# Attention: reciprocals of the softmax's sums carried over the partitions by DMA, outputs multiplied and split by GpSimd

## The chip, the cores and the metric

The kernel runs on one core of one Trainium2 chip. A core has a matrix engine (TensorE, PE in the profile; PEld is its loading of weights), three engines for elementwise work (VectorE or DVE, ScalarE or ACT, GpSimd or POOL), and a queue engine SP from which nearly all DMAs of this kernel are issued. Each engine executes its own list of instructions in order, and waits where an instruction needs what another engine has not finished. The metric is the device time of one execution in microseconds.

## The reference, cut to what matters

One layer over 1024 latent tokens and 256 context tokens, width 1024, all in float32: a gated feed-forward half-step, then a short convolution and grouped-query attention side by side, merged and projected, then a second half-step and a norm. The change lies in the attention of the latent tokens:

```python
def gqa_attend(q, k, v):
    s = jnp.einsum('btkgd,blkd->bkgtl', q, k, preferred_element_type=jnp.float32) * (HEAD_DIM ** -0.5)
    p = jax.nn.softmax(s, axis=-1).astype(v.dtype)
    return jnp.einsum('bkgtl,blkd->btkgd', p, v)
...
x = x + ml[5] * merge_branches(y_conv_l, o_l, gt_l, w_branch_conv[layer], w_branch_attn[layer], w_out[layer])
```

There are 8 query heads of 128 channels, 2 key and value heads, and 1280 keys (256 of the context, 1024 latent). The kernel multiplies the unnormalized sums of values by the reciprocal of the softmax's sum afterwards, and that is where the change is.

## The kernel before, in words

Every product that needs float32 precision is made of three faster ones: an operand is split into a high part and a low part (`split`, line 197: ACT casts the high part, then DVE, or POOL where it is named, subtracts it from the source), and `mm3` (line 229) does high times high, high times low and low times high.

The attention is cut into 16 units (`Unit`, line 1501): 8 heads by two halves `C0` and `C1` of 512 tokens. A unit does the following.

- `begin`: splits its queries into two tiles `qs` of 512 columns.
- `scores`, four times, for 128 queries each: nine matmuls against all keys, maxima by DVE (`m`, `nm`), exponentials by ACT into `pc` (context) and `pl` (latent), whose sums DVE adds into one column of `rsum`. So `rsum` is [128 queries of a block, 4 blocks]: the queries stand on the partitions.
- `turn`, ten times, for 128 keys each: four PE transposes put the keys on the partitions in a PSUM tile `pt`, and `split` makes `pts` of it. `pt` tiles come from `ps_t`, which has two PSUM banks.
- `values`, ten times: three matmuls of 512 columns add to `po` (one bank): [128 channels, 512 queries].
- `output` (line 1558): here the queries stand on the free axis, so the reciprocals `rinv`, one a partition, must be turned and repeated on all 128 partitions. The kernel does this by four PE transposes of a broadcast column into a `pt` bank; ACT copies `po` into the head's tile `q`, whose queries are no longer needed, and DVE multiplies it by the bank.

`seconds` (line 1568) runs turns and values of a unit behind the scores of the next; values follow their turn by `AHEAD` = 3. Between them `fillers` (line 1623) put the convolution branch's projection: weights `wc` (their low part by POOL), inputs `y`, gate `g`, result to DRAM as `zd`. From unit 13 on, `split_output` (line 1495) splits one finished head of 1024 columns, `q`, into `oh` and `ol` twice a unit; head 6 and the two halves of head 7 are split behind the units. `merge` (line 1591) then reads all eight heads' `oh` and `ol` in eight steps of three matmuls, with `ga` and `z` loaded from DRAM. The merges of the first two column blocks are woven into the last unit's turns. `later_mod` steps (`rawm` loads, `macc` on DVE) belong to the next feed-forward and are run behind the attention.

The order of the work is not written out by hand. A planner goes through the program and sets each engine's order from its own estimate of times: an instruction goes as soon as its inputs and a free buffer are there, the earlier in the program first. Only instructions marked as pinned or strict keep their place. So the scores run units ahead of the turns, and an instruction can appear well before its place in the text. The buffers that matter here: eleven tiles of 512 columns (`tpool`, by `ttile`), for `qs`, `g`, `ga`, `z`, `rawm`, `macc` and others; four of each kind of `small` tile, among them `rinv`; 38 of 1024 columns (`atile`) for `q`, `pl`, `oh`, `ol`.

In the profile, nearly all instructions carry line 90, that of a helper which issues them, so tiles are named rather than lines.

Of the kernel before, what the change touches and what calls it, by code (L numbers as in the profile page):

```python
# [9 lines left out]
F32 = mybir.dt.float32  # L10
# [8 lines left out]
P = 128  # L19
# [7 lines left out]
NQ = 8  # L27
# [8 lines left out]
C0, C1, CC = ("l", 0, 512), ("l", 512, 512), ("c", 0, CT)  # L36
# [15 lines left out]
def tile_dit_layer(  # L52
# [44 lines left out]
    act, dve, pool, pe, sp = (Engine(e) for e in (nc.scalar, nc.vector, nc.gpsimd, nc.tensor, nc.sync))  # L97
# [7 lines left out]
    dram = ctx.enter_context(tc.tile_pool(name="dram", bufs=1, space=DRAM))  # L105
# [3 lines left out]
    def uniq(s):  # L109
        n_tiles[0] += 1  # L110
        return f"{s}_{n_tiles[0]}"

    def atile(name, shape=(P, SLOT), dt=F32):
        return apool.tile(list(shape), dt, tag="A", name=uniq(name))

    def ttile(name, n=512, dt=F32):
        t = tpool.tile([P, 512], dt, tag="t", name=uniq(name))
        return t[:, :n]

    def small(name, n, dt=F32):  # L120
        return spool.tile([P, n], dt, tag=f"s{n}_{name}", name=uniq(name))
# [4 lines left out]
    def ps_t(n=512):  # L126
        return psum.tile([P, 512], F32, tag="t", name=uniq("pt"), bufs=2)[:, :n]
# [4 lines left out]
    def matmul(out, w, x, start, stop, pinned=False, on=False):  # L132

        inst = pe.matmul(out, w, x, start=start, stop=stop, skip_group_check=on)
        if pinned:
            tc.keep_in_program_order(inst)

    def transpose(out, in_, pinned=False):
        n = in_.shape[0]
        inst = pe.transpose(out, in_, ident[:n, :n])  # L140
        if pinned:
            tc.keep_in_program_order(inst)
# [43 lines left out]
    def col(name, k=0):  # L186
        o = voff[name] + k
        return cols[:, o : o + 1]
# [8 lines left out]
    def split(src, hi, lo, lo_eng=None, hi_eng=None):  # L197

        if hi_eng is dve:
            dve.tensor_copy(out=hi, in_=src)  # L200
        else:
            act.copy(out=hi, in_=src)
        (lo_eng or dve).tensor_sub(out=lo, in0=src, in1=hi.bitcast(F32))
# [257 lines left out]
    def run(steps, n=None):  # L461

        if n is None:
            for _ in steps:
                pass
        else:
            for _ in range(n):
                next(steps, None)
# [597 lines left out]
    for k in range(4):  # L1066
        if k % 2:
            half1.shifted(h0[k][:, 0], k, xh[k])
        else:
            dve.tensor_scalar(  # L1070
                out=h0[k][:, 0], in0=xh[k], scalar1=gain1["l"][:, k : k + 1], scalar2=modl[:, k : k + 1],
# [43 lines left out]
    hd = dram.tile([NH, P, L], F32, name="hd")  # L1115
# [78 lines left out]
    for j in range(NH):  # L1194
        half1.side = side(j) if j >= SIDE_FROM else None
        u, c = half1.next_first()
        v, b = half1.second(u)
# [20 lines left out]
    for d in range(0, KD, 2):  # L1218
        t = ttile("cx")
        src = cxd[d // 4, :, (d % 4) * CT : (d % 4 + 2) * CT]  # L1220
        sp.dma_start(out=t, in_=src)
        for e in range(2):
            te = t[:, e * CT : (e + 1) * CT]
            dve.scalar_tensor_tensor(
                out=te, in0=c_acc(d + e), scalar=gate1["c"][:, d + e : d + e + 1], in1=te, op0=ALU.mult, op1=ALU.add
# [71 lines left out]
    for i in range(KD):  # L1297
        u = atile("u")
# [5 lines left out]
        for ch, bg, gc in mixed():  # L1304
# [4 lines left out]
            for j in (0, 2):  # L1309
                a, b = max(o, 1 - j), min(o + 512, L + 1 - j)  # L1310
                ya = y[:, a - o : b - o]
                dve.scalar_tensor_tensor(
                    out=ya, in0=u[:, a + j - 1 : b + j - 1], scalar=col(f"w{j}", i), in1=ya, op0=ALU.mult, op1=ALU.add
# [112 lines left out]
    q_f = []  # L1426
# [65 lines left out]

    o_parts = [None] * NQ

    def split_output(hd, *chunks):
        if o_parts[hd] is None:
            o_parts[hd] = atile("oh", dt=F32R), atile("ol", dt=F32R)
        a, b = chunks[0][1], chunks[-1][1] + 512
        split(q_f[hd][:, a:b], *(t[:, a:b] for t in o_parts[hd]))

    class Unit:
        def __init__(self, hd, ch):
# [46 lines left out]
        def values(self, kt, pts):  # L1549
# [5 lines left out]
            matmul(po, vh, pts[:, 1], start=False, stop=False)  # L1555
            matmul(po, vl, pts[:, 0], start=False, stop=(kt == 9))

        def output(self):
            rinv = small("rinv", 4)
            of = q_f[self.hd][:, self.ch[1] : self.ch[1] + 512]  # L1560
            dve.reciprocal(out=rinv[:], in_=self.rsum[:])
            pr = ps_t()
            for qt in range(4):
                transpose(pr[:, qt * P : (qt + 1) * P], rinv[:, qt : qt + 1].to_broadcast([P, P]))
            act.copy(out=of, in_=self.po)
            dve.tensor_mul(out=of, in0=of, in1=pr)

    def seconds():

        turned = []  # L1570

        def value():
            u, kt, pts = turned.pop(0)
            u.values(kt, pts)
            if kt == 9:
                u.output()

        for u in units:
            for kt in range(10):
                turned.append((u, kt, u.turn(kt)))  # L1580
                if len(turned) > AHEAD:
                    value()
                yield
        while turned:
            value()
            yield
# [4 lines left out]
    def merge(j, ch):  # L1591

        if j not in m_hi:
            m_hi[j], m_lo[j] = atile("mh", dt=F32R), atile("ml", dt=F32R)
        if j not in wa:
            wa[j] = load_cols(w_ba[0], j * P)
        w, o = wa[j], ch[1]
        ga, z = ttile("ga"), ttile("z")
        sp.dma_start(out=ga, in_=gad[j, :, o : o + 512])
        sp.dma_start(out=z, in_=zd[j, :, o : o + 512])  # L1600
        ps = ps_s()
        terms = [
            (w[0][:, k], w[1][:, k], *(t[:, o : o + 512] for t in o_parts[k])) for k in range(KD)
        ]
        for k in range(KD - 1):
            mm3(ps, terms, k, k + 1)
            yield
        mm3(ps, terms, KD - 1)
        dve.tensor_mul(out=ga, in0=ga, in1=ps)
        dve.tensor_add(out=ga, in0=ga, in1=z)  # L1610
        split(ga, m_hi[j][:, o : o + 512], m_lo[j][:, o : o + 512])
        yield

    units = [Unit(hd, ch) for hd in range(NQ) for ch in (C0, C1)]
    u = units[0]
# [26 lines left out]
    for n_unit, u in enumerate(units[1:], 1):  # L1642
        u.begin()
        for n in (3, 2, 3, 2):
            u.scores(len(u.pl))
            for _ in range(n):
                run(rest, 1)
                if len(u.pl) < 4:
                    run(fill, 1)
            if n == 2:  # L1650
                run(fill, 1)
            if n == 2 and n_unit >= 13:
                split_output(next(to_split), C0, C1)
    run(fill)
    run(rest, 4)
    split_output(NQ - 2, C0, C1)
    split_output(NQ - 1, C0)
    merges = (step for j in range(2) for step in merge(j, C0))
    for _ in rest:
        run(merges, 2)  # L1660
    run(merges)
    split_output(NQ - 1, C1)


    for j in range(KD):
# [7 lines left out]
    for ch in (C0, C1):  # L1673
        o = ch[1]
        for d in range(KD):
# [7 lines left out]
                out=xs(d, ch), in0=ps, scalar=modl[:, 40 + d : 41 + d], in1=xs(d, ch), op0=ALU.mult, op1=ALU.add  # L1683
# [16 lines left out]
        out=gf[:], in0=cols[:, voff["gf"] : voff["gf"] + 8], scalar1=math.sqrt(D), scalar2=None, op0=ALU.mult  # L1700
# [46 lines left out]
    for j in range(NH):  # L1747
        if j > 1:
            run(last_steps, 3)
        u, c = fast.next_first()  # L1750
        v, b = fast.second(u)
# [81 lines left out]
```

## Time and profile before

| | us |
|---|---|
| three timed executions | 2706.02, 2708.07, 2708.09 |
| their median | 2708.07 |
| span of the profiled execution | 2709.4 |
| busy PE / DVE / ACT / POOL in it | 2656.2 / 2022.0 / 1179.3 / 512.0 |
| DMA mean rate | 138 GB/s |

The span is the profiled execution's own time from its first to its last instruction; no other time is listed for it. Its clock of the matrix engine was granted at a mean of 0.992. A busy matmul is pipelined with the next one: matmul durations overlap, and the time that a matmul takes from the engine is the distance from its start to the next one's. A row of a group gives its count, busy time, mean duration in ns, the idle time of its engine just before it, and what ended that idle time. A row of the timeline gives start, duration, engine, operation, and out<-in tiles.

### The profile page before, as it was taken

How to read it: one execution, taken by the hardware profiler on the slowest of the kernel's cores; microseconds unless marked ns; L12 is line 12 of the kernel's file. 1: busy time of each engine (PE TensorE's matmuls, PEld its weight loads, DVE VectorE, ACT ScalarE, POOL GpSimd, SP SyncE). 2: the span in 40 equal slices, each digit the busy share in tenths (PEclk: the TensorE clock that was granted, in tenths of full speed). 3: DMA queues.
4: the chain of work that ended last, by engine and by line, in shares of the span. 5: the costliest groups of instructions: out<-in, count | busy, mean ns of one | idle time of the engine just before them, and what ended most of it. 6: DMA issues, size and time to landing. Idle time of an engine off the chain costs nothing.

```text
span 2709.4 us, 37525 instructions
## 1 busy us (share of the span) xinstructions
PE 2656.2 (98%) x13685; PEld 2248.2 (83%) x13685; DVE 2022.0 (75%) x3387; ACT 1179.3 (44%) x2324; POOL 512.0 (19%) x403
## 2 busy tenths in 40 slices
PE   8999999999999999999999999999999999999998
PEld 6787899888778878888999888877888788888888
DVE  5788967788877898877387666685658876667885
ACT  6523444343443643333245666674236333334443
POOL 0144201111010034332033112000001442320200
PEclk9999999999999999999999999999999999999999
DMA  8565464335984355342313311011743552327831
GB/s 316 190 203 174 147 207 156 117 111 176 321 201 105 113 173 162 109 128 76 104 48 96 106 52 51 21 58 53 242 125 125 182 166 87 93 86 283 187 86 63
DMA packets 368209, 372.72 MB, mean 138 GB/s; under 512 B 18822, under 2 KB 257560, under 8 KB 368024
## 3 DMA queue, kind: packets, MB, share of 16 engines
q1 hardware_dynamic: 359000, 353.03, 39.5%
q0 software_dynamic: 9024, 17.30, 4.0%
q8 instruction: 107, 1.75, 0.3%
q14 instruction: 78, 0.64, 0.1%
HBM read 302.59 MB, written 67.63 MB: 137 GB/s over the span
## 4 chain that ended last, share of the span: by engine, by line
PE 56%; DVE 2%; ACT 0%; DMA 0%; issue 0%; DVEq 0%; SPq 0%; ACTq 0%
PE ps L90 47%; PE pt L90 5%; PE po L90 4%; DVE r L90 0%; DMA rawm<-in_w_mod_dram 0%; DVE ol L90 0%; DVE pts L90 0%; DVE m L90 0%; ACT pts L90 0%; DVE macc L90 0%; DVE nt L90 0%; DVE wl L90 0%; ACT oh L90 0%; ACT q L90 0%; ACT pc L90 0%
## 5 line engine op out<-in xcount | busy, mean ns | idle before, releaser
L90 PE MATMUL ps<-r,wl 128*128 128x512 f32 x5196 | 1207.3, 391 | 10.5 <-DVE wl L90 4.8
L90 PEld LDWEIGHTS ps<-r,wl 128*128 128x128 f32 x5196 | 974.7, 189 | 219.1 <-DVE wl L90 7.2
L90 ACT CAST wl<-s 128x512 fp32r<-128x512 f32 x254 | 157.1, 620 | 323.7 <-PE ps L90 235.3
L90 POOL TENSOR_TENSOR s<-raw 128x512 f32<-128x512 f32 x64 | 92.9, 1452 | 1065.2 <-DMA raw<-in_ffn_w_in_dram 410.3
L90 ACT CAST wl<-raw 128x512 fp32r<-128x512 f32 x287 | 177.5, 620 | 218.6 <-PE ps L90 159.6
L90 DVE TENSOR_TENSOR wl<-raw,wl 128x512 fp32r<-128x512 f32 x287 | 201.6, 705 | 64.6 <-ACT wl L90 62.2
L90 DVE TENSOR_TENSOR wl<-s,wl 128x512 fp32r<-128x512 f32 x254 | 231.0, 910 | 22.6 <-ACT wl L90 21.4
L90 POOL TENSOR_TENSOR s<-raw,s 128x512 f32<-128x512 f32 x64 | 102.1, 1595 | 364.9 <-DVE wl L90 364.9
L90 DVE SCALAR_TENSOR_TENSOR macc<-rawm,silu_c,macc 128x512 f32<-128x512 f32 x178 | 146.7, 842 | 29.0 <-DMA rawm<-in_w_mod_dram 28.3
L90 PE MATMUL ps<-wh,r 128*128 128x256 f32 x768 | 141.6, 285 | 0.0
L90 DVE TENSOR_TENSOR u<-u,ps 128x512 f32<-128x512 f32 x174 | 118.1, 679 | 30.6 <-PE ps L90 30.4
L90 DVE TENSOR_TENSOR pts<-pt,pts 128x512 fp32r<-128x512 f32 x160 | 108.5, 686 | 40.7 <-ACT pts L90 39.4
L90 ACT CAST pts<-pt 128x512 fp32r<-128x512 f32 x160 | 93.0, 593 | 89.0 <-PE pt L90 87.5
L90 DVE TENSOR_REDUCE m<-ps 128x1 f32<-128x512 f32 (+1 forms) x192 | 110.9, 595 | 27.6 <-PE ps L90 26.6
L90 ACT CAST rh<-hid 128x512 fp32r<-128x512 f32 x132 | 81.0, 620 | 106.7 <-PE ps L90 89.7
L90 PE MATMUL ps<-rh,wl 128*128 128x512 f32 x360 | 122.5, 392 | 2.8 <-ACT rh L90 2.8
L90 PEld LDWEIGHTS ps<-wh,r 128*128 128x128 f32 x768 | 120.6, 192 | 0.0
L90 PE MATMUL po<-pts,vh 128*128 128x512 f32 x256 | 110.9, 440 | 1.5 <-ACT pts L90 1.4
L90 ACT CAST wh<-raw 128x512 fp32r<-128x512 f32 (+1 forms) x85 | 67.8, 801 | 95.2 <-PE ps L90 59.3
L90 PE MATMUL ps<-wl,r 128*128 128x256 f32 x384 | 108.8, 283 | 0.0
L90 PE MATMUL ps<-kl,qs 128*128 128x512 f32 x384 | 106.1, 397 | 0.4 <-ACT pc L90 0.4
L90 DVE TENSOR_TENSOR rl<-hid,rh 128x512 fp32r<-128x512 f32 x132 | 90.1, 686 | 21.2 <-PE ps L90 10.8
(304 smaller groups left out, 5132.2 us busy)
## 6 DMA issues: line engine op xcount, KB each, us to landing
raw<-in_ffn_w_in_dram SPq DMA_DIRECT2D x130, 512.0 KB
raw<-in_ffn_w_out_dram SPq DMA_DIRECT2D x72, 512.0 KB
rawm<-in_w_mod_dram SPq DMA_DIRECT2D x136, 256.0 KB
raw<-in_w_in_dram SPq DMA_DIRECT2D x61, 512.0 KB
hid<-hd SPq DMA_DIRECT2D x40, 512.0 KB
ws<-in_ffn_w_out_dram POOLq DMA_DIRECT2D x30, 512.0 KB, 6.5
ucd<-uc SPq DMA_DIRECT2D x25, 512.0 KB
hd<-c SPq DMA_DIRECT2D x40, 256.0 KB
```

Source lines behind the costliest of these rows:

```text
L90: inst = getattr(self.engine, name)(*args, **kw)
```

## The change

`Unit.inverse` is new: DVE makes the reciprocals, SP stores their 128x4 values as one row of 512 in DRAM, each word on its own, and SP loads that row into all 128 partitions of a tile `rrow` of the pool of eleven. It stands behind the sixth of ten value steps. `output` loses the four transposes and the `pt` tile; its multiplication goes to POOL and reads `rrow`. `split_output` does both of its halves on POOL, a copy and a subtraction, but for the two halves of head 7, which stay on ACT and DVE.

```diff
-    def split_output(hd, *chunks):
+    def split_output(hd, *chunks, late=False):
         if o_parts[hd] is None:
             o_parts[hd] = atile("oh", dt=F32R), atile("ol", dt=F32R)
         a, b = chunks[0][1], chunks[-1][1] + 512
-        split(q_f[hd][:, a:b], *(t[:, a:b] for t in o_parts[hd]))
+        hi, lo = (t[:, a:b] for t in o_parts[hd])
+        if late:
+            split(q_f[hd][:, a:b], hi, lo)
+        else:
+            pool.tensor_copy(out=hi, in_=q_f[hd][:, a:b])
+            pool.tensor_sub(out=lo, in0=q_f[hd][:, a:b], in1=hi.bitcast(F32))
...
+        def inverse(self):
+            rinv = small("rinv", 4)
+            dve.reciprocal(out=rinv[:], in_=self.rsum[:])
+            row = dram.tile([512], F32, name=uniq("rinvd"))
+            sp.dma_start(out=row.rearrange("(j p) -> p j", p=P), in_=rinv[:])
+            self.rows = ttile("rrow")
+            sp.dma_start(out=self.rows, in_=row.partition_broadcast(P))
+
         def output(self):
-            rinv = small("rinv", 4)
             of = q_f[self.hd][:, self.ch[1] : self.ch[1] + 512]
-            dve.reciprocal(out=rinv[:], in_=self.rsum[:])
-            pr = ps_t()
-            for qt in range(4):
-                transpose(pr[:, qt * P : (qt + 1) * P], rinv[:, qt : qt + 1].to_broadcast([P, P]))
             act.copy(out=of, in_=self.po)
-            dve.tensor_mul(out=of, in0=of, in1=pr)
+            pool.tensor_mul(out=of, in0=of, in1=self.rows)
...
             u.values(kt, pts)
+            if kt == 5:
+                u.inverse()
             if kt == 9:
                 u.output()
...
     split_output(NQ - 2, C0, C1)
-    split_output(NQ - 1, C0)
+    split_output(NQ - 1, C0, late=True)
...
     run(merges)
-    split_output(NQ - 1, C1)
+    split_output(NQ - 1, C1, late=True)
```

## The prediction

> **What bounds the kernel now.** I read the page first, then the stretches around the attention, then the attention's groups, its chain and single rows.
>
> ```profile
> span 2709.4 us, 37525 instructions
> ...
> PE 2656.2 (98%) x13685; PEld 2248.2 (83%) x13685; DVE 2022.0 (75%) x3387; ACT 1179.3 (44%) x2324; POOL 512.0 (19%) x403
> ...
> PE   8999999999999999999999999999999999999998
> ...
> DVE  5788967788877898877387666685658876667885
> ...
> POOL 0144201111010034332033112000001442320200
> ...
> PE 56%; DVE 2%; ACT 0%; DMA 0%; issue 0%; DVEq 0%; SPq 0%; ACTq 0%
> ```
>
> Over the whole span the matrix engine (PE) is never short of work for long, and 56% of the chain that ended last is PE. The span is 2709.4 us; the three timed runs have a median of 2708.07, 1.3 us less. Differences are worked out on the profiled execution and taken off the median. What a timing of this kernel can tell from no change is about 0.2%, 5.4 us.
>
> The attention lies at about 1469 to 1885 us. Columns: stretch, its length, then busy time (and count) of each engine.
>
> ```profile
> core 0: us, PE busy (x) PEld busy (x) DVE busy (x) ACT busy (x) POOL busy (x), PEclk, DMA share, GB/s
> ...
> 1500.00:1540.00 40.00, 40.00 (x216) 33.48 (x216) 25.12 (x57) 25.55 (x66) 7.97 (x5) 1.00 0.30 92
> ...
> 1700.00:1740.00 40.00, 40.00 (x224) 33.68 (x223) 26.99 (x60) 23.68 (x62) 3.86 (x3) 1.00 0.06 21
> 1740.00:1780.00 40.00, 39.95 (x231) 33.77 (x231) 32.60 (x75) 31.06 (x83) 0.00 (x0) 1.00 0.12 40
> 1780.00:1820.00 40.00, 35.21 (x197) 27.97 (x196) 34.90 (x72) 29.50 (x74) 0.00 (x0) 0.99 0.19 60
> 1820.00:1860.00 40.00, 37.24 (x213) 29.59 (x214) 25.11 (x36) 19.83 (x34) 0.00 (x0) 0.97 0.04 14
> 1860.00:1900.00 40.00, 40.00 (x187) 33.12 (x186) 21.88 (x30) 13.07 (x20) 0.00 (x0) 1.00 0.35 105
> ...
> sum 480.00, PE 471.29 PEld 391.13 DVE 326.98 ACT 275.50 POOL 49.97; mean PE 39.27 PEld 32.59 DVE 27.25 ACT 22.96 POOL 4.16
> ```
>
> Up to 1780 PE is busy nearly without a break: a PE instruction taken out there shortens the run by its issue time, if what feeds PE keeps up. From 1780 to 1860 PE lacks 4.79 + 2.76 = 7.55 us; VectorE (DVE) is at 34.90 of 40 first, then the loop through one bank of turned scores binds: transposes, cast on ScalarE (ACT), subtraction on DVE, bank free. GpSimd (POOL) has no work at all from 1740 to 1860. After 1860 the merges' matmuls fill PE again.
>
> ```profile
> by line: PE ps L90 47.9%; PE po L90 23.2%; PE pt L90 16.8%; DMA rawm<-in_w_mod_dram 2.0%; DVE ol L90 1.6%; DVE pts L90 1.6%; DVE m L90 1.4%; ACT pts L90 0.9%; issue 0.9%; DVE macc L90 0.9%; ACT oh L90 0.6%; ACT q L90 0.6%; ACT pc L90 0.5%;
> ```
>
> In the 410 us of this chain DVE `ol` is 6.6 us, ACT `oh` 2.5 us, and the wait for `rawm` with `macc` 2.0% + 0.9%, 11.9 us.
>
> **The change part by part.** The groups of the attention's window that the edits touch, and those they are measured by (busy us, mean ns | idle before):
>
> ```profile
> L90 DVE TENSOR_TENSOR pts<-pt,pts 128x512 fp32r<-128x512 f32 x160 | 108.5, 686 | 40.7 <-ACT pts L90 39.4
> ...
> L90 ACT CAST pts<-pt 128x512 fp32r<-128x512 f32 x160 | 93.0, 593 | 89.0 <-PE pt L90 87.5 <-PE po L90 1.2
> ...
> L90 POOL TENSOR_TENSOR wc<-raw,wc 128x1024 fp32r<-128x1024 f32 x9 | 21.6, 2399 | 109.9 <-ACT wc L90 109.9
> ...
> L90 POOL TENSOR_TENSOR qs<-q,qs 128x512 fp32r<-128x512 f32 x13 | 17.5, 1347 | 97.5 <-ACT qs L90 62.6 <-PE ps L90 31.2 <-DMA zd<-g 3.7
> ...
> L90 DVE TENSOR_TENSOR q<-q,pt 128x512 f32<-128x512 f32 x16 | 10.9, 684 | 5.0 <-PE pt L90 4.8
> ...
> L90 PE MATMUL pt<-ident,rinv 128*128 128x128 f32 x64 | 9.6, 272 | 0.0
> ...
> L90 DVE TENSOR_TENSOR ol<-q,oh 128x1024 fp32r<-128x1024 f32 (+1 forms) x8 | 9.2, 1153 | 2.2 <-ACT oh L90 2.0 <-PE ps L90 0.2
> ...
> L90 ACT CAST oh<-q 128x1024 fp32r<-128x1024 f32 (+1 forms) x9 | 8.6, 960 | 4.1 <-DVE q L90 3.9 <-PE pt L90 0.2
> ...
> L90 DVE TENSOR_TENSOR wl<-raw,wh 128x1024 fp32r<-128x1024 f32 x4 | 4.9, 1223 | 0.7 <-ACT wh L90 0.6
> ```
>
> *1. The transposes of the reciprocals go: 64 on PE.* Their durations add up to 9.6 us, but matmuls overlap, so I take the issue time from successive starts:
>
> ```profile
> 1765.61 1.09 PE L90 MATMUL po<-pts,vc 128*128 128x512 f32 x4
> 1766.54 0.60 PE L90 MATMUL pt<-ident,rinv 128*128 128x128 f32 x4
> 1766.90 0.71 PE L90 MATMUL po<-pts,vc 128*128 128x512 f32 x2
> 1767.45 0.39 PE L90 MATMUL po<-pts,vh 128*128 128x512 f32 x1
> ```
>
> Four `po` matmuls take 1766.54 - 1765.61 = 0.93 us, 0.2325 each. From the start of the four transposes to the start of the row after the next two matmuls are 1767.45 - 1766.54 = 0.91 us; less 2 x 0.2325 leaves 0.445 us for four transposes. Sixteen units: **7.1 us of PE**. Most of them lie where PE has no break (PE's columns for this tile alone, by stretch):
>
> ```profile
> 1500.00:1780.00 280.00, 5.99 (x40) 4.88 (x40) 2.44 (x14) 1.00 0.17 55
> 1780.00:1860.00 80.00, 3.00 (x20) 2.45 (x20) 0.34 (x2) 0.98 0.12 37
> ```
>
> Forty come before 1780, twenty in the broken stretch. Bounds: 0 for those few that fall into PE's idle, 9.6 if nothing overlapped. I take 7.1, since the start-to-start difference is the nearest row. The product also held one of the two `pt` banks, which PE waits for:
>
> ```profile
> PEld pt L90 <- DVE pts L90: 8.7, 11, 2.3
> ...
> PE pt L90 <- DVE pts L90: 5.1, 8, 2.0
> ```
>
> That is 13.8 us of both queues together, mostly overlapping; part of the 7.55 us, so it isn't counted twice.
>
> *2. The multiplication moves from DVE to POOL: 16 x 0.684 us off DVE.* POOL has no row of a two-input product of this size in the window but `qs`, 1.347 us; I take 1.35 (bounds 1.28, its median, and 2.10, its longest, below). 16 x 1.35 = 21.6 us on an engine that has 50 of 480 us busy. Its result is read only by the head's split, and that only by the merges after 1860; so it costs the chain nothing until the last two units.
>
> *3. Seven splits of 1024 columns move from ACT and DVE to POOL.* Off ACT go 7 x 1.05 = 7.3 us, off DVE 7 x 1.22 = 8.5 us (one 512 piece of each group stays). On POOL the subtraction is `wc`, 2.40 us. A POOL copy of this size stands in no row: below, ACT's cast of the same shape, 1.05 us; above, POOL's two-input 2.40. I take 2.40, the same engine. Seven splits are 7 x 4.8 = 33.6 us on an engine that is empty for 120 us. The last of them, for head 6, must end before the merge's seventh step; its inputs come with the unit before the last two, so I cost it at 0; without that cover it would be 4.8 us.
>
> What the chain gets from 2 and 3: the 6.6 + 2.5 us of `ol` and `oh` leave it, and the matmuls cannot gain more there than PE's 7.55 us idle. What is late next is the cast and subtraction of `pts` (0.59 and 0.69 us a turn), and the `macc` steps, which stay. Bounds 0 and 7.55; I take about half, **4 us**, because DVE was full only in the first of the two stretches.
>
> *4. Two DMAs a unit on SP's queue, 32 in all: a scatter of 512 single words to DRAM and a broadcast of 2 KB to 128 partitions.* The second waits for the first, and everything behind on SP waits too: the next `raw` weights, `g`, `zd`, `ga`, `z`, `rawm`. The trace has no such pair. The nearest is the store and reload of `zd`:
>
> ```profile
> SPq L90 <- DVE g L90: 131.7, 10, 24.3
> ...
> SPq L90 <- DMA zd<-g: 17.0, 8, 3.2
> ```
>
> So a landing costs 2.1 us on average and 3.2 at the longest; lower bound 0.7 (two issues, if hidden), upper bound two landings, 6.4. I take 2 x 2.1 plus issues, 5 us, of which SP is held some 2.5. Against it stands the time from a reciprocal to its use:
>
> ```profile
> L90 PE MATMUL pt<-ident,rinv x64: 270/272/275, 1533.8 to 1871.3; 128*128 128x128 f32 x64
> L90 DVE RECIPROCAL rinv<-rsum x16: 158/178/179, 1502.7 to 1816.6; 128x4 f32<-128x4 f32 x16
> ```
>
> The first is 1502.7 to 1533.8, 31 us, the last 1816.6 to 1871.3, 55 us. The rows are in place 25 us and more before the product; SP itself idles up to 24.3 us at a time for DVE `g`. The reciprocal's 0.17 us is unchanged. Moving it to the sixth value tile instead of the tenth changes nothing, since the planner already runs it this early. Cost 0; bounds 0 and 16 x 2.5 = 40 us if each hold of SP reached PE.
>
> *5. The row takes a buffer of the pool of eleven* that `qs`, `g`, `ga`, `z` and `rawm` also use, from its load to the product: with a unit each (1871.3 - 1533.8) / 15 = 22.5 us and 28 to 52 us of life, two or three at a time. Until now the pool is filled with `qs` far ahead:
>
> ```profile
> L90 POOL TENSOR_TENSOR qs<-q,qs x16: 1276/1292/2097, 1472.2 to 1725.6; 128x512 fp32r<-128x512 f32 x16
> ```
>
> The last `qs` is made at 1725.6, 91 us before its unit's reciprocal at 1816.6. Shortening such a lead costs nothing until it falls under the 2 us that its cast and subtraction take. I take 0.
>
> *6. The last unit.* Its product takes 1.35 instead of 0.684 us: 0.7 us later, while the merge has seven of its eight steps of three matmuls (21 x 0.2325 = 4.9 us) to do before it reads that head. Cost 0, without that cover 0.7.
>
> The sum: -7.1 - 4 = -11.1 us, all else hidden: 2708.07 - 11.1 = **2697.0 us**, -0.41%.
>
> **Two rules weighed.** A two-input operation of DVE beside POOL:
>
> ```profile
> L90 DVE TENSOR_TENSOR modl<-mcol,bcol x14: 155/164/1252, 419.7 to 2323.0; 128x4 f32<-128x4 f32 x14
> ```
>
> A sum of 128x4 takes 0.16 us, and up to 1.25 us, a whole POOL operation more. The Trainium skill, "SBUF — State Buffer", section "Who interferes with whom", says that a VectorE instruction with two SBUF inputs contends with a GpSimd instruction that reads SBUF, that reductions never do, and that the loser blocks fully; this case's trace agrees by that row. The Trainium skill, "GPSIMD Engine Reference", section "4.1 Engine selection", keeps elementwise work off GpSimd as about twice as slow for two inputs; here it is 2.399 against 1.223 us, which agrees, and were all of it on the chain, by that rule it would be 16 x 0.67 + 7 x 2.5 = 28 us more, 2725. The trace has the engine idle where the work lands.
>
> **The rivals.**
>
> *A: the buffers decide (slower).* Rows, loads ahead and `qs` together fill the eleven buffers, a `qs` comes late, and PE waits at the next unit's first scores. For it: two or three more buffers are held, in order of the program. Against: 91 us of lead. It decides from 11.1 / 16 = 0.7 us a unit; at 1.3 us, the length of one late `qs` subtraction, 16 x 1.3 = 21 us: 2718.
>
> *B: the stall stays (no change that can be told).* What holds the stretch from 1780 is the loads of `rawm` and the bank's loop, not `ol`:
>
> ```profile
> L90 DVE SCALAR_TENSOR_TENSOR macc<-rawm,silu_c,macc x7: 741/750/753, 1796.7 to 1820.3; 128x512 f32<-128x512 f32 x7
> ...
>   DMA rawm<-in_w_mod_dram: 2.7, 3
> ```
>
> DVE stood 2.7 us for them, and 11.9 us of the chain. Then step 2 and 3 bring nothing, the five units used after 1780 bring nothing (5 x 0.445 = 2.2 us), and 7.1 - 2.2 = 4.9 us less some 2 us of such waits that come earlier remain: 2705.
>
> *C: POOL and DVE block each other.* The two-input work left beside POOL's 55 us more is 8 `macc`, 4 `wl` and some splits, about 20; if a quarter meet POOL for 1.1 us each, 5.5 us: 2702. For it: the row of 1.25 us. The rule of the Trainium skill's "SBUF — State Buffer" named above is the same. Against: `pts` and `m`, most of DVE's work here, read PSUM.
>
> *D: rows come late.* If SP were held by a `zd` store waiting for 24.3 us, the row would miss the product, and POOL's `qs` and `wc` stand behind that product. Against: 31 us of lead at the least. At 1.2 us a unit, near one `qs` subtraction, 16 x 1.2 = 19 us: 2716, slower.
>
> **How the numbers follow.** Forecast 0.66 (2688 to 2702.6: from every bound at its best, 7.1 + 7.55, with an allowance of 5 us for issue gaps that a busy row hides, to 0.2% under the median), C 0.05, B 0.15, A 0.10, D 0.04. Faster: 0.66 + 0.05 = 0.71; same: 0.15; slower: 0.14. The range runs from 2687 to 2710: it holds the forecast, C and B, and leaves out A and D and a little below.
>
> **What the changed profile would show.** Step 1: no `rinv` matmul, and PE busy time less by some 7 to 9 us before 1880. Step 2 and 3: POOL with 16 products of about 1.35 us and seven splits; no `oh` on ACT but two; PE's idle between 1780 and 1860 about halved. Step 4: two DMAs a unit on SP, landed 20 us or more before POOL's product; no PE wait that ends on a `raw` or `y` load and wasn't there. Step 5: no PE wait for `qs`. The prediction is wrong if PE waits for `qs`, if POOL's copy is far over 2.4 us so that the merges wait for `oh` or `ol`, or if the planner's other order of the same work costs PE more than 5 us somewhere after the attention.

## The result, and the profile after

The changed kernel takes 2717.18 us (median of 5 runs, 2716.7 to 2718.86) against 2708.07 us for the kernel before: a ratio of 1.0035, interval 1.0023 to 1.0047. Run once more (experiment 11), it gave 1.0029 (1.0018 to 1.0040). It is slower by some 8 to 9 us, where 11 us less were forecast.

From the page of the changed kernel, its span and the busy times:

```profile
span 2715.4 us, 37477 instructions
...
PE 2647.5 (98%) x13621; PEld 2237.8 (82%) x13621; DVE 2003.7 (74%) x3364; ACT 1170.6 (43%) x2317; POOL 553.6 (20%) x433
```

PE has 64 instructions fewer and is busy 8.7 us less, as step 1 said, yet the span is 6.0 us longer than in the profile before. So PE stands idle 14.7 us more. Where, the stretches of the changed kernel tell (busy time of PE is the first number after the length; the granted clock of PE stands behind POOL's count):

```profile
1540.00:1580.00 40.00, 36.35 (x188) 29.68 (x187) 25.60 (x57) 24.71 (x64) 4.98 (x3) 0.96 0.29 77
1580.00:1620.00 40.00, 37.49 (x182) 29.35 (x181) 22.20 (x46) 23.16 (x57) 8.13 (x6) 0.91 0.37 63
...
1780.00:1820.00 40.00, 40.00 (x234) 34.00 (x233) 30.06 (x69) 29.42 (x79) 17.63 (x13) 1.00 0.05 14
1820.00:1860.00 40.00, 26.44 (x142) 20.56 (x141) 19.46 (x33) 15.68 (x34) 11.60 (x7) 0.87 0.33 92
1860.00:1900.00 40.00, 39.38 (x194) 31.66 (x193) 21.99 (x30) 14.71 (x23) 2.74 (x2) 1.00 0.38 112
```

and the two stretches of the kernel before that the prediction didn't show:

```profile
1540.00:1580.00 40.00, 38.88 (x212) 32.02 (x211) 31.62 (x66) 28.39 (x70) 4.96 (x3) 1.00 0.24 80
1580.00:1620.00 40.00, 40.00 (x219) 33.86 (x218) 24.22 (x55) 24.76 (x62) 6.07 (x3) 1.00 0.19 60
```

From 1540 to 1620 PE now lacks 3.65 + 2.51 = 6.16 us, where it lacked 1.12. From 1780 to 1820 it lacks nothing, where it lacked 4.79, as was forecast. But VectorE's `macc` steps have left this stretch too (they started from 1793.9 to 1820.3, and now start from 1846.3 on), so it isn't shown that the moved splits and products did it. From 1820 to 1860 it lacks 13.56 us, where it lacked 2.76. The idle time isn't the whole loss: the granted clock is 0.91 from 1580 to 1620 and 0.87 from 1820 to 1860, where the kernel before had 1.00 and 0.97. Who waited for whom in the attention (us in total, times, longest):

```profile
DVE macc L90 <- DMA rawm<-in_w_mod_dram: 20.3, 7, 11.4
PEld pt L90 <- DVE pts L90: 16.7, 9, 11.4
PE pt L90 <- DVE pts L90: 13.4, 4, 10.9
ACT y L90 <- DMA y<-yd: 13.0, 4, 5.7
...
ACT oh L90 <- POOL q L90: 0.9, 1, 0.9
```

The longest single wait is VectorE's, 11.4 us at `macc` for a load of `rawm`. VectorE goes through its list in order, so the subtraction of the next `pts` stood behind it:

```profile
1834.19 0.69 DVE L90 TENSOR_TENSOR pts<-pt,pts 128x512 fp32r<-128x512 f32 x1 [0.45 <-ACT pts L90]
1846.29 0.49 DVE L90 TENSOR_SCALAR macc<-rawm,silu_c 128x512 f32<-128x512 f32 x1 [11.41 <-DMA rawm<-in_w_mod_dram]
1846.69 1.28 DVE L90 TENSOR_TENSOR pts<-pt,pts 128x512 fp32r<-128x512 f32 x2
```

Neither bank of turned scores comes free in these 12 us, and PE waits for `pts` as long (10.9 and 11.4 us at the longest). When PE starts again at 1847.43, it is slow at first:

```profile
1850.07 1.87 PE L90 MATMUL po<-pts,vc 128*128 128x512 f32 x4
1851.78 0.60 PE L90 MATMUL pt<-ident,pl 128*128 128x128 f32 x4
```

Four `po` matmuls take 1851.78 - 1850.07 = 1.71 us from start to start, where four took 0.93 in the prediction's rows. Why `rawm` was late, SP's list tells, the DMAs in order of their issue:

```profile
1827.50 0.37 SPq L90 DMA_DIRECT2D rinvd<-rinv  x1
1838.08 0.32 SPq L90 DMA_DIRECT2D rrow<-rinvd  x1
1838.49 0.38 SPq L90 DMA_DIRECT2D ga<-gad  x1
...
1840.39 11.34 SPq L90 DMA_DIRECT2D rawm<-in_w_mod_dram  x4
```

The store of the last unit's reciprocals is issued at 1827.50, and the load that needs it at 1838.08: SP stood 10.2 us for the landing, with `ga`, `z` and the loads of `rawm` behind. Sixteen such waits:

```profile
SPq L90 <- DMA rinvd<-rinv: 141.1, 16, 10.2
SPq L90 <- DVE rinv L90: 90.6, 15, 12.4
```

141.1 / 16 = 8.8 us for 2 KB. The second row is another wait of SP: the store itself waits at the head of SP's list until VectorE has made the reciprocals. The prediction didn't name it.

The store delays the convolution's inputs `y` too, between 1540 and 1620. ScalarE goes through its list in order like VectorE, and stands at `y` while the cast of the next `pts` is behind it; PE waits for that cast. A row of ScalarE, then one of PE:

```profile
1568.75 1.23 ACT L90 CAST y<-y 128x512 fp32r<-128x512 f32 x2 [4.87 <-DMA y<-yd]
```

```profile
1570.52 0.50 PE L90 MATMUL po<-pts,vh 128*128 128x512 f32 x1 [3.16 <-ACT pts L90]
```

SP's list there:

```profile
1550.24 0.43 SPq L90 DMA_DIRECT2D rinvd<-rinv  x1
1559.61 0.32 SPq L90 DMA_DIRECT2D rrow<-rinvd  x1
...
1560.93 3.25 SPq L90 DMA_DIRECT2D y<-yd  x4
1575.82 0.37 SPq L90 DMA_DIRECT2D rinvd<-rinv  x1
1576.28 5.82 SPq L90 DMA_DIRECT2D y<-yd  x4
```

The first four `y` loads go out only after the row's load at 1559.61, the other four right behind the next store at 1575.82, for whose reciprocals SP had stood 11.6 us, and their issue alone takes 5.82 us. In the kernel before all eight went out together:

```profile
1551.03 4.75 SPq L90 DMA_DIRECT2D y<-yd  x8
```

### The profile page after: what moved, and what is told of

The parts are those of the page before. It is cut to its first block, busy times and chain, and to the rows that moved or that the text cites. A ratio compares the mean times of both kernels' runs of the same rounds, so it can differ in the third digit from the quotient of the medians.

```text
span 2715.4 us, 37477 instructions
## 1 busy us (share of the span) xinstructions
PE 2647.5 (98%) x13621; PEld 2237.8 (82%) x13621; DVE 2003.7 (74%) x3364; ACT 1170.6 (43%) x2317; POOL 553.6 (20%) x433
## 2 busy tenths in 40 slices
DMA packets 378962, 376.96 MB, mean 139 GB/s; under 512 B 27526, under 2 KB 266264, under 8 KB 378776
## 4 chain that ended last, share of the span: by engine, by line
PE 86%; DVE 5%; issue 3%; DMA 3%; ACT 1%; POOL 1%; SPq 0%; DVEq 0%; POOLq 0%; ACTq 0%
PE ps L90 73%; PE pt L90 7%; PE po L90 7%; DMA rawm<-in_w_mod_dram 1%; DVE wl L90 1%; DVE r L90 1%; DVE macc L90 1%; DMA y<-yd 1%; SPq L90 0%; DVE nt L90 0%; DMA raw<-in_ffn_w_in_dram 0%; DMA ws<-in_ffn_w_out_dram 0%; DMA mcol<-mrow 0%; POOL s L90 0%; DMA hd<-u 0%
```

## The experiments

**1. The store by 16 bytes.** Theory 1 is the one that these rows suggest: SP held by the landing. Theory 2 is rival A, the buffer; theory 3 is rival C, POOL in VectorE's way.

```diff
-            sp.dma_start(out=row.rearrange("(j p) -> p j", p=P), in_=rinv[:])
+            sp.dma_start(out=row.rearrange("(p j) -> p j", j=4), in_=rinv[:])
...
-            pool.tensor_mul(out=of, in0=of, in1=self.rows)
+            of = of.rearrange("c (j p) -> c j p", p=P)
+            pool.tensor_mul(out=of, in0=of, in1=self.rows.rearrange("c (p j) -> c j p", j=4))
```

> The changed kernel, but the reciprocals go to DRAM as they lie, 16 bytes a partition (128 packets where there were 512 of 4 bytes), and GpSimd's product reads the row with a step of 4. Queue, buffers, waits and the order on SP stay nearly the same. Theory 1, SP is held by the landing of the word store (8.8 us each in the changed kernel) and the loads of y and rawm behind it come late: SP's wait for the store falls to 2 to 3 us each, VectorE's longest wait for rawm falls from 11.4 to under 5 us, and the time falls by 8 us or more, to 2700 to 2709. Theory 2, the buffer that a row holds pushes rawm behind the last row and that order alone costs: SP's wait falls all the same, but the time stays at 2714 to 2718. Theory 3, GpSimd's added work in VectorE's way: also 2714 to 2718, with GpSimd's products no shorter.

Measured: 2700.41 us, ratio 0.9977 (0.9968 to 0.9986). SP's wait and VectorE's, in that run:

```profile
SPq L90 <- DMA rinvd<-rinv: 21.4, 15, 2.5
```

```profile
DVE macc L90 <- DMA rawm<-in_w_mod_dram: 11.6, 7, 3.5
```

SP now waits 21.4 / 15 = 1.4 us for a store, less than the 2 to 3 expected, and the time is 14 to 16 us under the changed kernel's by the ratios: faster than the kernel before. Theory 1 holds; theories 2 and 3 predicted no change. SP's wait for the reciprocals is longer here than in the changed kernel, 139.0 us against 90.6, so that wait alone doesn't make the loss. The product that reads the row with a step of 4 costs POOL more, 1.563 us for 1.299, and nobody waits for it.

```profile
L90 POOL TENSOR_TENSOR q<-q,rrow 128x512 f32<-128x512 f32 x16 | 25.0, 1563 | 117.1 <-ACT q L90 117.1
```

**2. The load of the row later, the store as it is.** `inverse` is called one value step earlier and only stores; the load is put after the sixth value step and waits for that step's last matmul.

```diff
...
+        def fetch(self):
+            self.rows = ttile("rrow")
+            inst = sp.dma_start(out=self.rows, in_=self.row.partition_broadcast(P))
+            tc.add_manual_dep(
+                inst.ins, self.last.ins.name,
+                mybir.DependencyInfo(mybir.DependencyClass.Sync, mybir.DependencyReason.DATA), reason="late row",
+            )
...
-            if kt == 5:
+            if kt == 4:
                 u.inverse()
+            if kt == 5:
+                u.fetch()
```

> The changed kernel with the word store as it is, but the load of the row is made to wait for a value matmul of its own unit (the sixth of ten), so that the planner puts other DMAs between store and load and SP isn't held while the store lands. Theory 1: SP's waits for the store fall from 141 us to under 40, the y loads are issued earlier, time 2698 to 2708; what is left of the loss is where store and load still stand together at the end of the attention. Theory 2: the rows are held by their buffers for a shorter time, so a part comes back too, but the wait for rawm, which stands behind the last row, stays: 2710 to 2717. Theory 3: 2714 to 2718.

Measured: 2703.46 us, ratio 0.9987 (0.9979 to 0.9996).

```profile
SPq L90 <- DMA rinvd<-rinv: 45.4, 7, 8.8
```

```profile
ACT y L90 <- DMA y<-yd: 6.4, 2, 4.5
...
DVE macc L90 <- DMA rawm<-in_w_mod_dram: 5.6, 3, 3.1
```

SP waited 45.4 us for the store instead of 141.1, a little over the 40 expected, and VectorE 5.6 for `rawm` instead of 20.3. The store is as slow as before. SP still stands, now 85.3 us for the value matmuls. What is left of the loss lies elsewhere than expected: from 1540 to 1620, where `y` is still waited for (6.4 us), PE lacks 5.00 us, and at the end of the attention (1820 to 1860) only 1.35.

**3. No store at all.**

```diff
-            row = dram.tile([512], F32, name=uniq("rinvd"))
-            sp.dma_start(out=row.rearrange("(j p) -> p j", p=P), in_=rinv[:])
             self.rows = ttile("rrow")
-            sp.dma_start(out=self.rows, in_=row.partition_broadcast(P))
+            sp.dma_start(out=self.rows, in_=conv_w[0, 0, :512].partition_broadcast(P))
```

> The changed kernel without the store: every row is loaded from an input that is always there, so the division by the softmax's sum is left out (the reciprocal and the product by some row are still made). The buffer, the broadcast load and GpSimd's work are kept; only the store and the wait for its landing are gone. Theory 1: 2695 to 2703, the gain that was predicted. Theory 2 and theory 3: 2712 to 2718, since buffers and GpSimd's work are the same.

Measured: 2695.3 us, ratio 0.9957 (0.9946 to 0.9969), -0.43%: the gain that was forecast (-0.41%) is there when the store isn't. The buffer, the broadcast and POOL's work, all kept here, don't cost what the change lost. VectorE still waits for `rawm`, but never long:

```profile
DVE macc L90 <- DMA rawm<-in_w_mod_dram: 11.0, 7, 3.5
```

That the number agrees so well is in part luck. The prediction expected PE's idle time between 1780 and 1860 about halved; here it is 2.54 + 4.32 = 6.86 us, where it was 7.55:

```profile
1780.00:1820.00 40.00, 37.46 (x215) 31.05 (x215) 30.93 (x65) 28.64 (x77) 18.84 (x12) 1.00 0.15 46
1820.00:1860.00 40.00, 35.68 (x200) 27.79 (x199) 22.13 (x34) 17.81 (x30) 6.02 (x4) 1.00 0.25 72
```

**4. The splits alone**, put into the kernel before:

```diff
...
+        if late:
+            split(q_f[hd][:, a:b], hi, lo)
+        else:
+            pool.tensor_copy(out=hi, in_=q_f[hd][:, a:b])
+            pool.tensor_sub(out=lo, in0=q_f[hd][:, a:b], in1=hi.bitcast(F32))
...
```

> The kernel before with one part of the change alone: the seven splits on GpSimd (a copy and a subtraction of 1024 columns each). Theory 1: no DMA is added, so a gain of 0 to 6 us from VectorE and ScalarE: 2702 to 2708. Theory 3, GpSimd's work costs by itself: over 2710.

Measured: 2702.5 us, ratio 0.9987 (0.9978 to 0.9996), 3.9 us less by the medians, 1 to 6 by the interval. PE lacks 3.36 + 1.53 = 4.9 us where it lacked 7.55:

```profile
1780.00:1820.00 40.00, 36.64 (x207) 29.86 (x205) 32.97 (x67) 25.10 (x65) 10.65 (x7) 0.96 0.21 61
1820.00:1860.00 40.00, 38.47 (x222) 30.95 (x222) 22.46 (x33) 18.38 (x32) 3.42 (x2) 1.00 0.08 26
```

**5 and 6. The `macc` steps kept in place**, once with the 16-byte store and once with the word store of the change. The first `macc` of each half may not be moved ahead of VectorE's instructions before it in the program, so none stands in the attention.

```diff
+                    strict[0] = k == 0 and m in (6, 7)
                     if k == 0:
                         dve.tensor_scalar(out=acc, in0=raw, scalar1=s, scalar2=None, op0=ALU.mult)
...
+                    strict[0] = False
```

> The kernel with 16-byte stores (e1), and the first macc step of each column half of the next feed-forward's modulation is kept in its place in VectorE's list, behind the merge before it, so that no macc waits for rawm in the attention's last stretch. If what PE still lacks there (5.7 us between 1820 and 1860 in that run) is VectorE standing at macc for rawm (11.6 us), PE's idle there falls under 2.5 us and the time by 2 to 6 us against e1: 2694 to 2699. If the bank's loop of pts is what binds, nothing changes: 2699 to 2702.

Measured: 2692.9 us, ratio 0.9942 (0.9927 to 0.9957), the lowest of all and a little under what was expected, though its interval overlaps those of experiments 3, 6 and 7. PE lacks 1.32 us in the two stretches together, where it lacked 0.71 + 5.67 in experiment 1:

```profile
1780.00:1820.00 40.00, 40.00 (x231) 33.91 (x230) 30.21 (x69) 31.11 (x84) 21.28 (x13) 1.00 0.11 28
1820.00:1860.00 40.00, 38.68 (x221) 30.88 (x220) 22.70 (x36) 20.75 (x39) 10.41 (x6) 1.00 0.19 54
```

> The changed kernel with its word store, and the same first macc steps kept in place. It takes away the 11.4 us wait of VectorE at macc behind which the turned scores stood, and leaves SP held for 8.8 us a unit. If that wait is the larger part of the loss: 2703 to 2709, with the loss between 1540 and 1620 (6.2 us of PE idle) left. If SP's hold costs elsewhere: over 2712.

Measured: 2699.38 us, ratio 0.9963 (0.9951 to 0.9975), faster than expected. SP is held nearly as long as in the changed kernel, and from 1540 to 1620 most of the loss is left, 2.58 + 2.39 = 4.97 of 6.16 us; the last stretch is mended:

```profile
SPq L90 <- DMA rinvd<-rinv: 118.7, 15, 9.3
```

```profile
1540.00:1580.00 40.00, 37.42 (x200) 30.43 (x199) 27.09 (x61) 27.07 (x72) 4.98 (x3) 1.00 0.33 78
1580.00:1620.00 40.00, 37.61 (x189) 29.50 (x189) 23.73 (x49) 22.94 (x55) 9.90 (x6) 0.96 0.31 68
1820.00:1860.00 40.00, 38.82 (x224) 31.13 (x224) 22.26 (x37) 21.84 (x43) 11.22 (x8) 1.00 0.24 69
```

So the largest part of the loss hung on one store, the last, and it took two things: loads held behind the store, and an instruction that was not due yet standing in VectorE's list and waiting for them.

**7. The store by 16 bytes and the load later.** The edits of 1 and 2 together.

> Both ways at once: 16-byte stores, and the row's load behind a value matmul of its unit. SP's wait for the store is then near 0. If 1.4 us a unit of SP's hold still cost something in e1: 2694 to 2699. If not, the same as e1 or, since SP now waits for matmuls, up to 3 us more: 2700 to 2704.

Measured: 2697.0 us, ratio 0.9958 (0.9946 to 0.9970). That lies in the range for a hold that still cost something, but its interval overlaps that of experiment 1 (0.9968 to 0.9986) by little; whether the late load adds anything to the short store isn't settled.

**8. Words of a partition side by side.** 512 packets of 4 bytes as in the change, at other addresses. The edit also writes these buffers once at the start of the kernel, and the row that is loaded is the first half of the words.

```diff
-            row = dram.tile([512], F32, name=uniq("rinvd"))
-            sp.dma_start(out=row.rearrange("(j p) -> p j", p=P), in_=rinv[:])
+            row = rinvd[2 * self.hd + (self.ch[1] > 0)]
+            sp.dma_start(out=row[:, :, 0], in_=rinv[:])
             self.rows = ttile("rrow")
-            sp.dma_start(out=self.rows, in_=row.partition_broadcast(P))
+            sp.dma_start(out=self.rows, in_=row.rearrange("p j o -> (p j o)")[:512].partition_broadcast(P))
...
+    rinvd = [dram.tile([P, 4, 2], F32, name=f"rinvd{i}") for i in range(16)]
+    for i in range(16):
+        sp.dma_start(out=rinvd[i].rearrange("p j o -> (p j o)"), in_=x[0, i])
```

> 512 words of 4 bytes a store as in the changed kernel, but a partition's four words lie together in DRAM, 8 bytes apart, where the changed kernel puts neighbouring partitions' words side by side; the row that is loaded is then not the right one, so the division by the softmax's sum is wrong. If the number of packets sets the landing, SP's wait is 8 to 10 us again. If many partitions writing into the same few bytes of DRAM set it, the wait falls to 2 to 4 us.

One execution, 2707.36 us.

```profile
SPq L90 <- DMA rinvd<-rinv: 53.6, 16, 5.4
```

53.6 / 16 = 3.4 us a store: less than half of 8.8 with the same number of packets and bytes, more than the 1.4 us of 128 packets. So the number of packets doesn't set the landing alone. 3.4 lies inside the range expected if it matters which partitions' words are neighbours in DRAM; but the form of the access differs too (512 rows of one word instead of 128 of four), so the address isn't shown to be the cause.

**9. The kernel before with `macc` in place.** The edit of 5, in the kernel before.

> The kernel before, with only the first macc steps kept in place. It tells how much of e5's and e6's gain belongs to the change and how much the kernel before could have had without it. In the kernel before VectorE waited 2.7 us for rawm and PE lacked 7.55 us in that stretch: if the macc steps were the cause, 2700 to 2705; if not, within 2 us of before.

Measured: 2704.27 us, ratio 0.9993 (0.9985 to 1.0002): nothing that can be told from no change, though the median lies in the first range. PE lacks 2.09 + 3.15 = 5.24 us in the two stretches, and 4.89 with the splits alone (experiment 4): neither alone empties them, as experiment 5 does. What 5 and 6 gained doesn't come from keeping `macc` in place alone.

**10. All three**: 16 bytes, late load, `macc` in place.

> 16-byte stores, the row's load behind a value matmul, and the first macc steps kept in place. If the late load still takes something that e5 lacks: 2689 to 2692. If SP's 1.4 us a unit are hidden: the same as e5, 2691 to 2696.

Measured: 2697.45 us, ratio 0.9968 (0.9957 to 0.9979): outside both ranges, not better than experiment 5, rather a little worse. SP waits 124.0 us for the value matmuls here, and PE lacks 0.49 + 0.74 + 1.05 + 1.35 = 3.63 us from 1700 to 1860, where experiment 5 lacks 1.32. So the late load seems to have a price of its own.

**11. The changed kernel again.**

> The changed kernel itself once more, on the same chip as the others of this call, so that its distance to them has no chip between: 2713 to 2719.

Measured: 2713.27 us, ratio 1.0029 (1.0018 to 1.0040).

**12. Experiment 5 with the splits back** on ScalarE and VectorE, against experiment 5:

```diff
-        if late:
-            split(q_f[hd][:, a:b], hi, lo)
-        else:
-            pool.tensor_copy(out=hi, in_=q_f[hd][:, a:b])
-            pool.tensor_sub(out=lo, in0=q_f[hd][:, a:b], in1=hi.bitcast(F32))
+        split(q_f[hd][:, a:b], hi, lo)
```

> e5 with the seven splits back on ScalarE and VectorE as in the kernel before. If moving them to GpSimd is worth what the splits alone gave to the kernel before (3.9 us), e5's time plus 2 to 5 us: 2695 to 2699. If GpSimd's splits matter only where VectorE also stood at macc, the same as e5.

Measured: 2697.16 us, inside the first range, ratio 0.9968 (0.9956 to 0.9980), against 0.9942 (0.9927 to 0.9957) with the splits on POOL: 7 us by the ratios, between some 0 and 14 by the ends of the intervals. PE lacks 3.69 + 1.48 = 5.17 us from 1780 to 1860, where experiment 5 lacks 1.32.

## Why the prediction was wrong, point by point

**Steps 1 and 2 held, step 3 in part.** POOL's rows of the changed kernel:

```profile
L90 POOL TENSOR_TENSOR q<-q,rrow 128x512 f32<-128x512 f32 x16 | 20.8, 1299 | 129.0 <-ACT q L90 129.0
...
L90 POOL TENSOR_TENSOR ol<-q,oh 128x1024 fp32r<-128x1024 f32 x7 | 16.7, 2391 | 7.6 <-PE pt L90 7.2
...
L90 POOL CAST oh<-q 128x1024 fp32r<-128x1024 f32 x7 | 7.3, 1038 | 0.1
```

The product takes 1.299 us (1.35 forecast), the subtraction 2.391 (2.40). The copy takes 1.038 us, just under the lower end of 1.05 to 2.40 from which I took the upper: POOL reading one input of 1024 columns takes about as long as ScalarE's cast. The splits alone gave 3.9 us by the medians (4 forecast for them and the products). Of PE's idle time at the end of the attention the splits took away 7.55 - 4.89 = 2.66 us in the kernel before (experiment 4) and 5.17 - 1.32 = 3.85 us where `macc` is kept out of the attention (experiments 12 and 5). With no store the whole change gave 0.43% (0.41% forecast), but the idle time stayed at 6.86 us there, so that number doesn't confirm step 3.

**Step 4 is the one that failed.** It said: a landing costs 2.1 us, so SP is held for some 2.5 us a unit, and the row has 25 us and more to spare. The row had less at first, and enough all the same: from the issue of the load to the start of the product there are 19.3 us in the first unit (1512.4 to 1531.7) and 54 in the last (1838.1 to 1892.5), and POOL's idle time before the products ends on ScalarE's `q`, never on a row.

```profile
L90 SPq DMA_DIRECT2D rrow<-rinvd x16: 319/320/333, 1512.4 to 1838.1; - x16
L90 POOL TENSOR_TENSOR q<-q,rrow x16: 1276/1290/1451, 1531.7 to 1892.5; 128x512 f32<-128x512 f32 x16
```

But the landing took 8.8 us and not 2.1, and the time to spare is the row's own. It doesn't cover what is queued behind the waiting load on SP. I named those (`raw`, `g`, `zd`, `ga`, `z`, `rawm`) and then priced them by the row's cover, at 0. `y`, for which ScalarE waited 13.0 us, isn't in that list. The price was taken from the landing of 256 KB in large packets, as the nearest row; for 512 single words it was four times too low. The term's bounds, 0 and 40 us, held the truth: between the changed kernel's ratios, 1.0035 and 1.0029, and experiment 1's 0.9977 lie 14 to 16 us, and to experiment 3's 0.9957, where no store is left, 19 to 21. That is far less than the 141.1 us of SP's waiting: most of it cost nothing.

The Trainium skill, "DMA: Bandwidth & Descriptors", section "Rules for kernel authors", says that a strided last dimension lowers to one descriptor per element and should be rearranged to be contiguous. The runs agree in part. Against experiment 3 the page of the changed kernel counts (27526 - 19078) / 16 = 528 packets under 512 bytes a store more, that of experiment 1 (21382 - 19078) / 16 = 144, and SP waits 8.8 and 1.4 us. But experiment 8, where the last dimension is strided too, has 3.4 us.

**Steps 5 and 6 were small.** No wait of PE for `qs` appears. ScalarE waited 0.9 us for the product of one unit of head 7 (`oh` in the fence of waits above), and PE lacks only 0.62 us from 1860 to 1900.

**Rival D named the right queue and the wrong victim.** It let the row come too late for its product. What came too late were the loads behind it. No forecast had a place for that. That D's 2716 us and A's 2718 lie next to the measured 2717.18 is luck: neither mechanism is in the trace.

**Rival A, the buffers, falls as the cause,** since experiment 3 keeps them and gains 0.43%. It may have a share in it: in the changed kernel the last row, then `ga` and `z`, then `rawm` are issued in the program's order, from 1838 on. Without the store the first `rawm` is issued at 1811.2, still later than in the kernel before, 1775.1:

```profile
L90 SPq DMA_DIRECT2D rawm<-in_w_mod_dram x8: 328/333/384, 1775.1 to 1816.5; - x8
```

In the changed kernel that order put these loads right behind the last store. How the time would go with more buffers wasn't tried.

**Rival B saw the place, not the size.** It took 2 us for more waits of `macc` for `rawm`; there were 20.3 us of them, 11.4 in one. Keeping `macc` in place gives back more than the loss (experiment 6, 0.9963).

**Rival C falls as the cause.** POOL's work is nearly the same in experiments 1, 3 and 5, and all are faster than the kernel before. But what it says does happen: in the changed kernel one `macc`, which has both inputs in SBUF, starts at 1852.99 and takes 2.487 us instead of 0.753, while POOL's subtraction `ol` runs from 1852.56 for 2.37, and PE then waits 1.93 us for `pts`. What it costs in all wasn't measured.

## What to carry to other kernels

A DMA that waits for another DMA on the same queue holds everything queued behind it until the landing, however early its own result is. That costs time only where a load behind it is due: price it by the next loads in that queue, and ask who stands waiting for them, in order, on which engine. The store of single words was slow to land here; one contiguous piece for each partition, with the stride left to the reader, landed sooner. Work that a planner pulls ahead into an engine that looks idle does harm when its input comes late; where its load moves behind something slow, keep it in its place.

## What the runs showed of the hardware

The store of 128 partitions by 4 words took 8.8 us of SP's waiting when neighbouring partitions' words were adjacent in DRAM, 3.4 us when a partition's four words were, and 1.4 us as 128 pieces of 16 bytes, all for 2 KB. After 10.93 us without a matmul, PE took 1.71 us for four matmuls of 512 columns that take 0.93 otherwise, and its granted clock from 1820 to 1860 was 0.87. POOL's copy of 128x1024 from float32 takes 1.038 us (1.097 in experiment 1) where its two-input subtraction takes 2.391. POOL's product with one input read at a step of 16 bytes takes 1.563 us instead of 1.299.
